# Down projections in parts of 6, 8 and 8 pairs, and the table of attention bias made during layer 0's up projection

## The chip, the cores and the metric

The kernel runs on one core of one Trainium2 chip. The metric is the device time of one execution in microseconds (us). Three runs of the kernel before took 1335.24, 1335.5 and 1338.54 us; their median, 1335.5, is the time that the change is measured against.

## The reference, cut to what matters

A trunk of two layers, for one sequence of 512 tokens of width 1024, all in fp32. Layer 0 is a Mamba-2 mixer and a ConvFFN. Then keys and values are projected once. Layer 1 is a differential attention over them, and a ConvFFN. Two pieces bear on the change: the ConvFFN of both layers (FFN width 2816), and the attention's table of bias, which depends on the distance of two tokens alone.

```python
def conv_ffn(x, ln_g, up_w, conv_w, conv_b, down_w):
    u = causal_dwconv(rms_norm(x, ln_g) @ up_w, conv_w, conv_b)
    gate, up = u[..., :FFN_DIM], u[..., FFN_DIM:]
    return (jax.nn.silu(gate) * up) @ down_w
...
    dist = qpos[:, None] - kpos[None, :]
    bias = rel_bias[t5_bucket(dist)].astype(jnp.float32).transpose(2, 0, 1)
    logits = jnp.einsum('bqhcd,bkhcd->bhcqk', qblk, k).astype(jnp.float32) * scale
    logits = logits + bias[None, :, None]
    logits = jnp.where(dist >= 0, logits, -jnp.inf)
...
        ff = conv_ffn(x, ffn_ln_g[layer], ffn_up_w[layer], ffn_conv_w[layer],
                      ffn_conv_b[layer], ffn_down_w[layer])
        x = x + ff.astype(x.dtype)
```

rel_bias has 32 buckets for each of 8 heads; t5_bucket gives every distance up to 15 a bucket of its own and shares the others out by ranges.

## The kernel before, in words

**Products.** TensorE (PE) multiplies in fp32r. For fp32 accuracy each operand is split into a high half (wh, xgh, sh) and a low half (wl, xgl, sl), and each product is made of three: wh·xh, wh·xl and wl·xh (helper mm3, L205 to L208). The halves of a weight chunk are made on the chip: ScalarE (ACT) writes the high half with a copy, VectorE (DVE) the low half with a subtraction.

**The order of the weights.** A list written at the start, `plan` (L69 to L120), names every weight chunk in the order in which PE will use it. `chunk(key)` hands out the next one and sees to it that two more (AHEAD = 2) are already split behind it. A raw chunk is loaded on SyncE's (SP's) queue into one of three buffers.

**The ConvFFN.** `ffn(l, ...)` (L954) serves both layers. The FFN's 2816 columns are 22 "pairs", each 128 gate and 128 up columns. Pairs come in parts (`PARTS_D`, L32: 8, 8 and 6). For each pair of a part, PE makes the gate and up products from two weight chunks, 48 matmuls; DVE and ACT apply the convolution's taps (L977 to L982), SiLU (L1223) and the multiplication (L1227); then `operands` (L1052 to L1080) forms, for each two pairs (a "quad"), seven sums of halves of the activations for a Strassen-like product, each in a high and a low half (sh, sl). Their buffers hold four quads.

Behind a part's last pair comes its down product. Instead of eight block products it makes seven, in the order of `SEVEN` (L33): 5, 1, 2, 6, 7, 4, 3 in layer 0 and 1, 2, 5, 7, 6, 3, 4 in layer 1. In layer 0 `down_features` (L1160) makes each of the seven from two weight chunks (14 chunks in a part), in banks of PSUM named ps_s; its matmuls are at L1186, L1188 and L1189, 6 for each quad and chunk and half of columns, so 24 a chunk with four quads and 18 with three. DVE adds the finished products to the residual stream xT (L1168) and to a running sum (L1205). In layer 1 `down_tokens` (L1082) does the same by tokens, adds to xr (L1100), and in the last part cuts the very last product (L1094, banks `end`) and stores the output as it goes.

**The down weights.** For the seven products sums of weight blocks are needed. `ahead` (L1010), called at the third pair of a part, marks the buffers behind that pair's activations (POOL copies, L1016), loads a block on SP's queue (L1017), and adds a second block to it with accumulating DMAs on GpSimd's (POOL's) queue (`plus`, L1007). `combine` (L1021) splits such a sum when its turn in `plan` comes (ACT L1035, DVE L1036) and then issues the next accumulation into the same buffer wz, for a later product. The accumulations for the first products of a part are thus issued while the up products run, and the one for the part's fourth product behind the split of the first.

**The end of layer 0.** In its last part each finished piece of xT calls `ended`: ACT and DVE split it for the key projection (xgh, xgl, L500 to L503), ACT squares it (L576), POOL sums the squares (L577) and DVE folds them (nacc_kv, L579), for the key norm, which a short chain of small DVE operations ends (L511, then L257 to L265).

**The transition into layer 1.** `proj` (L1262) multiplies the key, query and value weights, four token banks at a time, with chunks wr_k, wr_q, wr_v whose halves are made at L171 and L172. `qk` (L1285) empties each bank (ACT, knk L1293), squares it into one buffer (ACT, ksq L1294) and sums the squares (DVE, ssk L1295). Ahead of this, when the attention section begins, the table of bias is made: rb is loaded on POOL's queue (L1245), POOL copies its 32 columns into the ranges of distance, 18 copies in two tiles bv (L1255), and two DMAs on the same queue write it to the DRAM tile bd (L1256). For each head `Unit.logits` loads the table's rows from bd in a shifted form on SP's queue (tr, L1339, one buffer), and DVE reverses them into tb (L1340, two buffers).

**Who orders what.** Each engine runs its instructions in the order in which the scheduler has put them; a wait at the head of an engine's row holds all that is behind it. The same holds for the DMA issues on SP's and POOL's queues.

Of the kernel before, what the change touches and what calls it, by code (L numbers as in the profile page):

```python
# [9 lines left out]
F32 = mybir.dt.float32  # L10
# [8 lines left out]
P = 128  # L19
# [9 lines left out]
FFN = 2816  # L29
NPAIR = FFN // P  # L30
HALF = 12
PARTS_D = (0, 8), (8, 16), (16, 22)  # L32
SEVEN = "5126743", "1257634"  # L33
AH = 8
EPS = 1e-6
NEG = -1.0e30
LAM_INIT = 0.8 - 0.6 * math.exp(-0.3 * 1)
NBIAS = 640
# [3 lines left out]
def trunk_kernel(ctx: ExitStack, tc, x, ssm_ln_g, ssm_in_w, ssm_conv_w, ssm_conv_b, ssm_dt_bias,  # L42
# [4 lines left out]
    act, dve, pool, pe, sync = nc.scalar, nc.vector, nc.gpsimd, nc.tensor, nc.sync  # L47
# [9 lines left out]
    dp = ctx.enter_context(tc.tile_pool(name="scratch", bufs=1, space=DRAM))  # L57
# [33 lines left out]
    def ffn_plan(l):  # L91
        for p0, p1 in PARTS_D:
            for p in range(p0, p1):
                plan.append(("g%d_%d" % (l, p), *w_cols(ffn_up_w[l], 0, KB, p * P, P)))
                plan.append(("u%d_%d" % (l, p), *w_cols(ffn_up_w[l], 0, KB, FFN + p * P, P)))
            nq = (p1 - p0) // 2
            for m in SEVEN[l]:
                for c in range(0, nq, 2) if l else range(2):
                    plan.append(("s%d%s_%d_%d" % (l, m, p0, c), (l, m, p0, c, min(2, nq - c) if l else nq)))
# [168 lines left out]
    with tc.tile_pool(name="ph0", bufs=1) as p0:  # L268
# [153 lines left out]
        for l in range(2):  # L422
            for j in range(2):
                sfc = slice(j * FFN, (j + 1) * FFN)
                d = sf[:, 2 * l + j, :]
# [525 lines left out]
        run(out_proj(NG - 1, *prev, norm))  # L951


    def ffn(l, norm, bp, gnext, nnext):  # L954
        with tc.tile_pool(name="ffn_h%d" % l, bufs=1) as hp, tc.tile_pool(name="ffn%d" % l, bufs=1) as fp:
            rr = []

            def products(j, p, c=None):
                key = "%s%d_%d" % ("gu"[j], l, p)
                wh, wl = chunk(key)  # L960
                ps = mm_bank("ps_" + key)
                for k in range(KB):
                    last = mm3(ps, wh[:, k, :], wl[:, k, :], xgh[k], xgl[k], k == 0, k == KB - 1)
                    if c is not None and k == KB - 2:
                        with tc.issue_after(last):
                            rr.append(norm.row(c))
                return ps

            def taps(j, p, ps):
                key = "%s%d_%d" % ("gu"[j], l, p)  # L970
                r = rr[0]
                col = lambda t: cf[l][:, 88 * j + 22 * t + p:88 * j + 22 * t + p + 1]
                u = fp.tile([P, T], F32, tag="u", name="u" + key, bufs=3)
                v = fp.tile([P, T], F32, tag="v%d" % j, name="v" + key, bufs=3 if j else 4)
                if nnext is None and key in ("g1_1", "u1_1"):
                    residual(j)
                dve.tensor_tensor(out=u, in0=ps, in1=r, op=ALU.mult)  # L977
                act.activation(v, u, AF.Identity, bias=col(3), scale=col(2))
                for s in range(1, 3):
                    dve.scalar_tensor_tensor(out=v[:, s:], in0=u[:, :T - s], scalar=col(2 - s),  # L980
                                             in1=v[:, s:], op0=ALU.mult, op1=ALU.add)
                return v  # L982
# [16 lines left out]
            def source(p0, c, nq, j, i):  # L999
                p0, i = (p0 + 2 * c, i) if l else (p0, 2 * c + i)  # L1000
                src = ffn_down_w[l][p0 * P:(p0 + 2 * nq) * P, i * ncol:(i + 1) * ncol]
                return src.rearrange("(k j p) c -> j p k c", j=2, p=P)[j]

            def view(t, nq):
                return t[:, :nq * ncol].rearrange("p (k c) -> p k c", k=nq)

            def plus(t, p0, c, nq, j, i):  # L1007
                pool.dma_start(view(t, nq), source(p0, c, nq, j, i), accum_op=ALU.add)  # L1008

            def ahead(p0, n, behind):  # L1010

                for k, j, i in (("z", 0, 0), ("x", 0, 1), ("y", 1, 1)) if l else (("x", 0, 0), ("z", 0, 1)):
                    for c in range(0, n // 2, 2) if l else range(2):
                        nq = min(2, n // 2 - c) if l else n // 2
                        t = raws[k][c // 2 if l else c]
                        pool.tensor_copy(t[:, 0:1], behind[:, 0:1])  # L1016
                        sync.dma_start(view(t, nq), source(p0, c, nq, j, i))  # L1017
                        if k == "z" and not l:
                            plus(t, p0, c, nq, 1, 1)
# [195 lines left out]

            for p0, p1 in PARTS_D:
                sides = []
                for p in range(p0, p1):
                    ps = [products(0, p)]
                    if not rr:  # L1220
                        ps.append(products(1, p, norm.col()))
                    ga = taps(0, p, ps[0])
                    act.activation(ga, ga, AF.Silu)  # L1223
                    if len(ps) == 1:
                        ps.append(products(1, p))
                    up = taps(1, p, ps[1])
                    dve.tensor_tensor(out=ga, in0=ga, in1=up, op=ALU.mult)  # L1227
                    operands(p, ga, sides)
                    if p == p0 + 2:
                        ahead(p0, p1 - p0, ga)  # L1230
                (down_tokens if nnext is None else down_features)(p0, p1 - p0, sides, p1 == NPAIR)

    norm_kv = Norm(bp, "kv")
    ffn(0, norm, bp, None, norm_kv)


    norm1 = Norm(bp, "f1")
    with tc.tile_pool(name="att_o", bufs=1) as op_, tc.tile_pool(name="att", bufs=1) as ap:
        rts = []
        late = []  # L1240


        rb = ap.tile([AH, 32], F32, name="rb")
        bd = dp.tile([AH, NBIAS], F32, name="bd")
        pool.dma_start(rb, rel_bias.rearrange("b h -> h b"))  # L1245
        hb = NBIAS // 2
        for i in range(2):
            bv = ap.tile([AH, hb], F32, tag="p1", name="bv%d" % i, bufs=3)
            if i == 0:
                pool.memset(bv[:, 0:P - 1], NEG)  # L1250
            for b, a, e in _ranges():
                a, e = max(a - i * hb, 0), min(e - i * hb, hb)
                if a < e:
                    src = rb[:, 0:e - a] if b == 0 else rb[:, b:b + 1].to_broadcast([AH, e - a])
                    pool.tensor_copy(bv[:, a:e], src)  # L1255
            pool.dma_start(bd[:, i * hb:(i + 1) * hb], bv)  # L1256

        kT = [ap.tile([P, 4, T], F32, name="kT%d" % i) for i in range(2)]
        qT = [ap.tile([P, 4, T], F32, name="qT%d" % i) for i in range(2)]
# [213 lines left out]
        with tc.manual_schedule(engines={mybir.EngineType.PE}):  # L1473
# [90 lines left out]
            last_out(norm1)  # L1564

    ffn(1, norm1, bp, None, None)


def _ranges():
    dist = np.arange(NBIAS - (P - 1))  # L1570
    nf = np.maximum(dist, 1).astype(np.float32)
    large = 16 + (np.log(nf / np.float32(16)) / np.float32(math.log(8)) * np.float32(16)).astype(np.int32)
    bucket = np.where(dist < 16, dist, np.minimum(large, 31))
    at = P - 1 + np.searchsorted(bucket, np.arange(33))
    return [(0, P - 1, int(at[16]))] + [(b, int(at[b]), int(at[b + 1])) for b in range(16, 32)]
# [27 lines left out]
```

## Time and profile before

| | |
|---|---|
| runs of before (us) | 1335.24, 1335.5, 1338.54; median 1335.5 |
| the profiled execution's own time | 1335.32 us |
| its span (first to last instruction) | 1333.4 us |
| instructions | 18218 |
| TensorE clock granted | 1.00 throughout |
| layer 0's up products and down parts | from 376.9 to 730.2 us, with the down parts beginning at 464.8, 592.2 and 697.8 us |
| key, query and value projections and attention | from 730.2 us |
| layer 1's last down part | 1297.7 us to the end |

A line of the profile gives times in us from the span's start or as sums. In a group of instructions "out<-in" are the names of the tiles in the program, then come partitions x elements, a count, and in square brackets or behind the bar the idle time of that engine just before, with the instruction that ended it. A line "PE ps_q L1271 <- ACT knk L1293: 3.2, 1, 3.2" of the waits says who waited, for what, the sum of its idle time, how often, and the longest. A line of the transfers gives the size and the median time from issue to landing. A line of a table of stretches begins with the stretch and its length, and then has busy time and number of instructions of PE, PE's weight loads, DVE, ACT and POOL, the granted clock, the DMA share and GB/s.

### The profile page before, as it was taken

Reading aid. Unit: us, or ns where it says so; the run is one execution under the profiler, and the core shown is the slowest. Engines: PE = TensorE matmul, PEld = TensorE weight load, DVE = VectorE, ACT = ScalarE, POOL = GpSimd, SP = SyncE. Lnnn points to the kernel's source line nnn. Section 1 sums busy time; section 2 is a strip of 40 time slices with the busy share of each in tenths; the row PEclk is TensorE's granted clock in tenths of the full one; section 3 lists DMA queues with packets and bytes.
Section 4 is the critical chain, followed back from the end, with each engine's and each line's share of the span. In section 5 each row is a group of like instructions: output and inputs, shape, how many; then the busy total and the mean of one; then the engine's idle time right before and its main releaser. Section 6 shows DMA issues by size and latency. Waiting matters only on the chain.

```text
span 1333.4 us, 18218 instructions
## 1 busy us (share of the span) xinstructions
PE 1318.6 (99%) x6795; PEld 1100.3 (83%) x6795; DVE 1074.8 (81%) x1814; ACT 700.5 (53%) x1150; POOL 153.1 (11%) x210
## 2 busy tenths in 40 slices
PE   9999999999999999999998899999999999999998
PEld 8878888888888898889888787777788888888886
DVE  7989888789878886888789556777777987888788
ACT  6696553752444443544446455777654443454443
POOL 4330300200111010111013200000020010001001
PEclk9999999999999999999999999999999999999999
DMA  7553533432337463745365432221136353544444
GB/s 207 161 151 96 147 99 111 135 95 72 95 94 180 104 129 111 190 95 130 108 147 107 119 98 85 73 78 56 54 89 187 97 112 101 184 111 80 126 134 111
DMA packets 196024, 155.25 MB, mean 116 GB/s; under 512 B 7196, under 2 KB 175520, under 8 KB 195936
## 3 DMA queue, kind: packets, MB, share of 16 engines
q1 hardware_dynamic: 173904, 120.73, 30.8%
q0 software_dynamic: 20752, 32.26, 12.8%
q8 instruction: 53, 0.87, 0.3%
q10 hardware_dynamic: 1280, 1.10, 0.3%
q14 instruction: 35, 0.29, 0.1%
HBM read 151.83 MB, written 2.25 MB: 116 GB/s over the span
## 4 chain that ended last, share of the span: by engine, by line
PE 89%; DVE 6%; DMA 2%; ACT 1%; issue 1%; POOL 0%; SPq 0%; DVEq 0%; ACTq 0%
PE ps_g L207 5%; PE ps_u L207 5%; PE ps_u L206 5%; PE ps_g L208 5%; PE ps_g L206 5%; PE ps_u L208 5%; PE ps_in L206 5%; PE ps_in L208 5%; PE ps_in L207 5%; PE ps_s L1188 2%; PE ps_s L1189 2%; PE ps_s L1186 2%; PE ps_s L1094 2%; PE ps_o L207 2%; PE ps_o L206 2%; PE ps_o L208 2%
## 5 line engine op out<-in xcount | busy, mean ns | idle before, releaser
L206 PE MATMUL ps_u<-xgh,wh_u 128*128 128x512 f32 x352 | 137.4, 390 | 0.0
L207 PE MATMUL ps_g<-xgl,wh_g 128*128 128x512 f32 x352 | 137.1, 389 | 0.0
L206 PE MATMUL ps_g<-xgh,wh_g 128*128 128x512 f32 x352 | 137.1, 389 | 0.0
L208 PE MATMUL ps_u<-xgh,wl_u 128*128 128x512 f32 x352 | 137.0, 389 | 0.0
L208 PE MATMUL ps_g<-xgh,wl_g 128*128 128x512 f32 x352 | 137.0, 389 | 0.0
L207 PE MATMUL ps_u<-xgl,wh_u 128*128 128x512 f32 x352 | 137.0, 389 | 0.0
L206 PE MATMUL ps_in<-xgh,wh_in 128*128 128x512 f32 x304 | 123.0, 404 | 0.0
L208 PE MATMUL ps_in<-xgh,wl_in 128*128 128x512 f32 x304 | 119.8, 394 | 0.0
L207 PE MATMUL ps_in<-xgl,wh_in 128*128 128x512 f32 x304 | 119.2, 392 | 0.0
L207 PEld LDWEIGHTS ps_g<-xgl,wh_g 128*128 128x128 f32 x352 | 66.2, 188 | 13.9 <-DVE xgl L486 0.3
L208 PEld LDWEIGHTS ps_u<-xgh,wl_u 128*128 128x128 f32 x352 | 66.1, 188 | 13.8
L1189 PE MATMUL ps_s<-sl,wh_s 128*128 128x256 f32 x308 | 77.4, 283 | 0.0
L1188 PE MATMUL ps_s<-sh,wh_s 128*128 128x256 f32 x308 | 77.4, 283 | 0.0
L206 PEld LDWEIGHTS ps_g<-xgh,wh_g 128*128 128x128 f32 x352 | 66.1, 188 | 13.7
L208 PEld LDWEIGHTS ps_g<-xgh,wl_g 128*128 128x128 f32 x352 | 66.1, 188 | 13.6
L207 PEld LDWEIGHTS ps_u<-xgl,wh_u 128*128 128x128 f32 x352 | 66.1, 188 | 13.5
L206 PEld LDWEIGHTS ps_u<-xgh,wh_u 128*128 128x128 f32 x352 | 66.1, 188 | 13.5
L1008 POOL DMA_DIRECT2D wz<-in_ffn_down_w_dram x36 | 43.7, 1255 | 290.3 <-DVE wl_s L1036 224.2
L1079 ACT ACTIVATE sh<-vg 128x256 fp32r<-128x256 f32 (+1 forms) x44 | 23.0, 524 | 98.2 <-DVE vg L1227 98.1
L1223 ACT ACTIVATE vg<-vg 128x512 f32<-128x512 f32 x44 | 27.8, 633 | 88.6 <-DVE vg L980 88.6
L977 DVE TENSOR_TENSOR uu<-ps_u,nr_f 128x512 f32<-128x512 f32 x44 | 30.4, 691 | 52.3 <-PE ps_u L208 52.2
L146 ACT ACTIVATE wh_u<-wr_u 128x1024 fp32r<-128x1024 f32 x44 | 46.7, 1062 | 44.0 <-PE ps_g L207 36.1
(398 smaller groups left out, 3509.0 us busy)
## 6 DMA issues: line engine op xcount, KB each, us to landing
wr_g<-in_ffn_up_w_dram SPq DMA_DIRECT2D x44, 512.0 KB, 3.9
wr_u<-in_ffn_up_w_dram SPq DMA_DIRECT2D x44, 512.0 KB, 3.9
wr_in<-in_ssm_in_w_dram SPq DMA_DIRECT2D x40, 512.0 KB, 3.9
wz<-in_ffn_down_w_dram POOLq DMA_DIRECT2D x27, 512.0 KB, 6.5
m<-cumd POOLq DMA_DIRECT2D x16, 512.0 KB, 4.7
wr_out<-in_ssm_out_w_dram SPq DMA_DIRECT2D x16, 512.0 KB, 3.5
wr_s<-in_ffn_down_w_dram SPq DMA_DIRECT2D x13, 512.0 KB, 3.8
xT<-in_ffn_down_w_dram SPq DMA_DIRECT2D x10, 512.0 KB, 7.7
```

The lines of the kernel that those rows point to most:

```text
L146: return act.activation(self.wh[:, :self.n], self.raw[:, :self.n], AF.Copy)
L206: pe.matmul(ps, wh, xh, start=start, stop=False)
L207: pe.matmul(ps, wh, xl, start=False, stop=False)
L208: return pe.matmul(ps, wl, xh, start=False, stop=stop).ins
L977: dve.tensor_tensor(out=u, in0=ps, in1=r, op=ALU.mult)
L1008: pool.dma_start(view(t, nq), source(p0, c, nq, j, i), accum_op=ALU.add)
L1079: act.activation(sh[:, o], v, AF.Copy)
L1094: pe.matmul(pss[b], h, ws[q][1][:, cols], start=False, stop=end and q == qs[-1])
L1186: pe.matmul(v[:, b], wl[:, q, cols], h, start=False, stop=q == nq - 1)
L1188: pe.matmul(v[:, b], wh[:, q, cols], h, start=q == 0, stop=False)
L1189: pe.matmul(v[:, b], wh[:, q, cols], w, start=False, stop=False)
L1223: act.activation(ga, ga, AF.Silu)
```

## The change

Two edits. The parts of the down projection are 6, 8 and 8 pairs in place of 8, 8 and 6, in both layers. And the making of the bias table leaves the attention section for layer 0's ConvFFN, where it is called behind the fourth pair (p = 3); it is held until that pair's activations are there by a copy of one of their columns into rb, on POOL, ahead of rb's load. Its tiles rb and bv now lie in the ConvFFN's pool; bv has two tiles of its own.

```diff
-PARTS_D = (0, 8), (8, 16), (16, 22)
+PARTS_D = (0, 6), (6, 14), (14, 22)
...
+    bd = dp.tile([AH, NBIAS], F32, name="bd")
+
+    def bias_ranges(pl, behind):
+        rb = pl.tile([AH, 32], F32, name="rb")
+        pool.tensor_copy(rb[:, 0:1], behind[:AH, 0:1])
+        pool.dma_start(rb, rel_bias.rearrange("b h -> h b"))
+        hb = NBIAS // 2
+        for i in range(2):
+            bv = pl.tile([AH, hb], F32, name="bv%d" % i)
+            if i == 0:
+                pool.memset(bv[:, 0:P - 1], NEG)
+            for b, a, e in _ranges():
+                a, e = max(a - i * hb, 0), min(e - i * hb, hb)
+                if a < e:
+                    src = rb[:, 0:e - a] if b == 0 else rb[:, b:b + 1].to_broadcast([AH, e - a])
+                    pool.tensor_copy(bv[:, a:e], src)
+            pool.dma_start(bd[:, i * hb:(i + 1) * hb], bv)
...
                     if p == p0 + 2:
                         ahead(p0, p1 - p0, ga)
+                    if not l and p == 3:
+                        bias_ranges(fp, ga)
...
-        rb = ap.tile([AH, 32], F32, name="rb")
-        bd = dp.tile([AH, NBIAS], F32, name="bd")
-        pool.dma_start(rb, rel_bias.rearrange("b h -> h b"))
...
-            bv = ap.tile([AH, hb], F32, tag="p1", name="bv%d" % i, bufs=3)
...
-            pool.dma_start(bd[:, i * hb:(i + 1) * hb], bv)
```

The lines of the changed kernel lie 18 further in ffn and 4 further in the attention section (L1016 is L1034, L1036 is L1054, L1340 is L1344).

**POOL at the third and fourth pair of layer 0.** Before, the marking copies of `ahead` (for wz_1 the last of four) are followed by the accumulations, first those of the first products (2 rows), then those issued behind the splits:

```order
L1016 COPY wz_1_3660<-vg_2_3893 128x1
L1008 DMA wz_0_3659<-in_ffn_down_w_dram 128x4x256
L1008 DMA wz_1_3660<-in_ffn_down_w_dram 128x4x256
L1008 DMA wz_0_3659<-in_ffn_down_w_dram 128x4x256
L1008 DMA wz_1_3660<-in_ffn_down_w_dram 128x4x256
```

Now, in the changed kernel, the table stands there (rb's marking copy, its load, the 18 copies, of which the first and the last are shown, and the two DMAs to bd):

```order
L1034 COPY wz_1_3661<-vg_2_3894 128x1
L1026 DMA wz_0_3660<-in_ffn_down_w_dram 128x3x256
L1026 DMA wz_1_3661<-in_ffn_down_w_dram 128x3x256
L958 COPY rb<-vg_3_3988 8x1
L959 DMA rb<-in_rel_bias_dram 8x32x1
L969 COPY bv_4042<-rb 8x16
...
L969 COPY bv_4062<-rb 8x320
L970 DMA bd<-bv_4042 8x320
L970 DMA bd<-bv_4062 8x320
L1026 DMA wz_0_3660<-in_ffn_down_w_dram 128x3x256
L1026 DMA wz_1_3661<-in_ffn_down_w_dram 128x3x256
```

The table has moved ahead of the accumulations for the first part's fourth product; those have three quads in place of four. From POOL's row behind the key norm's last sum (nsum, L577) it is gone. Only the memset of bv's first tile goes further ahead, to layer 0's norm before the ConvFFN.

**DVE at the beginning of the key projection.** Before, from the last small operation of the key norm (tr_nkv, L265), with the weight splits for the query projection (wl_q), the two reversed copies of the table (tb) and the first sum of squares of the keys (ssk):

```order
L265 SCALAR_TENSOR_TENSOR tr_nkv<-rst_nkv,tr_nkv 128x4
L172 SCALAR_TENSOR_TENSOR wl_q_0_6990<-wr_q_0_6987,c_89,wh_q_0_6989 128x512 x2
L1340 COPY tb_7384<-tr_7385 128x512
L172 SCALAR_TENSOR_TENSOR wl_q_2_7022<-wr_q_2_7019,c_89,wh_q_2_7021 128x512 x2
L1340 COPY tb_7539<-tr_7540 128x512
L1295 TENSOR_REDUCE ssk_6896<-ksqk_0_7040 128x8
```

In the changed kernel, from the fold of the key norm's last sums (nacc_kv) and the last key split on:

```order
L579 TENSOR_TENSOR nacc_kv<-nsum_3665 128x256
L172 SCALAR_TENSOR_TENSOR wl_k_4_6937<-wr_k_4_6934,c_89,wh_k_4_6936 128x512 x2
L1344 COPY tb_7385<-tr_7386 128x512
L511 TENSOR_REDUCE tr_nkv<-tr_nkv 128x4
...
L265 SCALAR_TENSOR_TENSOR tr_nkv<-rst_nkv,tr_nkv 128x4
L1344 COPY tb_7540<-tr_7541 128x512
L172 SCALAR_TENSOR_TENSOR wl_q_0_6991<-wr_q_0_6988,c_89,wh_q_0_6990 128x512 x2
L172 SCALAR_TENSOR_TENSOR wl_q_2_7023<-wr_q_2_7020,c_89,wh_q_2_7022 128x512 x2
L1299 TENSOR_REDUCE ssk_6897<-ksqk_0_7041 128x8
```

The first copy of the table stands ahead of the key norm's reduction (L511), the second ahead of both query splits; before, both stood behind the norm, between and behind the query splits. On SP the load of the first tr now stands ahead of that of the query weights' third chunk (wr_q_4), before it stood behind.

**DVE at the end of layer 0's last down part.** Before, with three quads, the last two splits of down weights (wl_s, 768 elements) and what lies between and behind them: additions to xT and the low halves of the finished pieces (xgl):

```order
L1036 TENSOR_TENSOR wl_s_16_0_6726<-wz_0_3659,wh_s_16_0_6725 128x768
L503 TENSOR_TENSOR xgl<-xT,xgh 128x2x256
L1168 TENSOR_TENSOR xT<-xT,ps_s_16_0_6729 128x2x256
L1036 TENSOR_TENSOR wl_s_16_1_6755<-wz_1_3660,wh_s_16_1_6754 128x768
L1168 TENSOR_TENSOR xT<-xT,ps_s_16_1_6758 128x2x256
```

Now, with four:

```order
L1054 TENSOR_TENSOR wl_s_14_0_6729<-wz_0_3660,wh_s_14_0_6728 128x1024
L503 TENSOR_TENSOR xgl<-xT,xgh 128x2x256
L1186 TENSOR_TENSOR xT<-xT,run_sum_3666 128x2x256 x2
L1186 TENSOR_TENSOR xT<-xT,ps_s_14_0_6732 128x2x256
L503 TENSOR_TENSOR xgl<-xT,xgh 128x2x256
L1054 TENSOR_TENSOR wl_s_14_1_6764<-wz_1_3661,wh_s_14_1_6763 128x1024
L503 TENSOR_TENSOR xgl<-xT,xgh 128x2x256
```

The last splits have 1024 elements in place of 768; the additions of a finished running sum stand behind the split of 14_0 where they stood ahead of it, and otherwise the rows are the same.

PE's rows have the same matmuls as before, up to the parts: 252 in each layer 0 part of six pairs and 336 in each of eight.

More of the change, by code (lines that the diff above doesn't have):

```diff
@@ L1240, in trunk_kernel @@
         late = []
-        rb = ap.tile([AH, 32], F32, name="rb")
-        bd = dp.tile([AH, NBIAS], F32, name="bd")
-        pool.dma_start(rb, rel_bias.rearrange("b h -> h b"))
-        hb = NBIAS // 2
-        for i in range(2):
-            bv = ap.tile([AH, hb], F32, tag="p1", name="bv%d" % i, bufs=3)
[L1249 to L1256, printed above, removed]
         kT = [ap.tile([P, 4, T], F32, name="kT%d" % i) for i in range(2)]
```

## The prediction

> **What bounds the kernel.** I read the page first, for the busy time of each engine.
>
> ```profile
> span 1333.4 us, 18218 instructions
> PE 1318.6 (99%) x6795; PEld 1100.3 (83%) x6795; DVE 1074.8 (81%) x1814; ACT 700.5 (53%) x1150; POOL 153.1 (11%) x210
> ```
>
> PE is busy for 1318.6 of 1333.4 us. The change leaves PE every matmul it had (order prints 6002 rows for PE before and after), so there are only 15 us of idle PE and the tail behind its last matmul to win. The view of waits says whom PE waits for.
>
> ```profile
> PE ps_q L1271 <- ACT knk L1293: 3.2, 1, 3.2
> PE ps_k L1272 <- DVE wl_k L172: 2.7, 2, 1.7
> PE ps_s L1186 <- DVE wl_s L1036: 1.6, 2, 0.9
> ...
> PE ktk L1309 <- issue: 0.4, 1, 0.4
> ```
>
> These are 7.9 us in six waits, and in order of time they stand within 45 us: the end of layer 0's last down part (ps_s L1186), the first key projection (ps_k), the first query projection (ps_q, ktk). Each wait costs a little more than its idle time, for a matmul runs 0.39 us and the next one normally starts 0.23 us after it: 0.16 us of overlap are lost each time, 1.0 us in all. **Layer 0's end costs 8.9 us.** The columns of the next rows, of the down parts' instructions alone, are the stretch, its length, and busy time with the number of instructions of each engine.
>
> ```profile
> 465.00:505.00 40.00, 40.00 (x335) 40.00 (x335) 10.19 (x15) 1.16 (x2) 1.00 0.64 129
> 697.80:730.20 32.40, 30.73 (x252) 30.28 (x252) 9.51 (x14) 1.18 (x2) 1.00 0.58 117
> 1069.20:1107.20 38.00, 38.00 (x168) 31.30 (x167) 8.98 (x14) 1.18 (x2) 1.00 0.49 95
> 1297.70:1328.30 30.60, 29.46 (x123) 22.32 (x122) 8.87 (x14) 1.17 (x2) 1.00 0.47 95
> ```
>
> A part of eight pairs runs without a gap: 0.119 us a matmul in layer 0, 0.226 in layer 1. A part of six, which here is each layer's last, does not: 252 matmuls at 0.119 are 30.0 us and take 32.4; in layer 1, 123 at 0.226 and six half-width ones at 0.12 are 28.5 and take 30.6, so 2.1 us are lost there too, most of it too short for the list of waits.
>
> **The bias table.** Its stall is seen in DVE's rows behind the key projection, with ACT's and POOL's beside them.
>
> ```profile
> 740.87 0.41 DVE L579 TENSOR_TENSOR nacc_kv<-nsum 128x256 f32<-128x256 f32 x1
> ...
> 742.30 0.69 DVE L511 TENSOR_REDUCE tr_nkv<-tr_nkv 128x4 f32<-128x512 f32 x1 [0.35 <-PE tr_nkv L509]
> ...
> 745.85 1.42 DVE L172 SCALAR_TENSOR_TENSOR wl_q<-wr_q,c,wh_q 128x512 fp32r<-128x512 f32 x2 [0.48 <-ACT wh_q L171]
> 755.92 0.43 DVE L1340 COPY tb<-tr 128x512 f32<-128x512 f32 x1 [8.65 <-DMA tr<-bd]
> ```
> ```profile
> 751.89 0.69 ACT L1293 ACTIVATE knk<-ps_k,tr_nkv 128x512 f32<-128x512 f32 x1
> ...
> 760.55 0.63 ACT L1294 ACTIVATE ksqk<-knk 128x512 f32<-128x512 f32 x1 [6.66 <-DVE ssk L1295]
> ```
> ```profile
> 742.05 0.78 POOL L1245 DMA_DIRECT2D rb<-in_rel_bias_dram  x1 [4.18 <-DVE wl_k L172]
> ...
> 746.52 3.13 POOL L1255 COPY bv<-rb 8x16 f32<-8x16 f32 x18 [3.51 <-DMA rb<-in_rel_bias_dram]
> 749.61 1.08 POOL L1256 DMA_DIRECT2D bd<-bv  x2
> ```
> ```profile
> wz<-in_ffn_down_w_dram POOLq DMA_DIRECT2D x6, 384.0 KB, 6.5
> tr<-bd SPq DMA_DIRECT2D x8, 256.0 KB, 3.1
> ```
>
> POOL cannot begin the table before 742.05 and hands it over at 750.7; the copy of its first rows holds DVE's queue 8.65 us. Behind it stand the sums of squares (ssk); ACT, which empties the key banks (knk) and squares them (ksqk), has one buffer for the squares and waits 6.66 us, so a bank of key products is not emptied, and PE waits its 3.2 us. With the table made 300 us earlier, this chain has no start: the 3.2, the 0.4 of ktk behind it and two overlaps, 3.9 us, go.
>
> Is DVE free of the copy now? In the new order the first copy stands ahead of the norm's reduction (order rows above). Its load may start when the norm's last sums (nacc_kv) are done, at 741.3 in the old time, and takes 3.1 us (the median, last row): 744.4. The copy's 0.43 end at 744.8. The reduction it holds up stood at 742.30, with small operations behind it until 745.4; 2.5 us later they end at 747.9. The first key bank is emptied at 751.89, so 4 us are spare, and more when layer 0's end loses less. On SP the weight load wr_q_4 stands behind that load; it asks for a buffer that the last key split frees at about the same time. I count nothing, with the old 3.9 us as the other end.
>
> **The parts in layer 0.** What makes the last part late is DVE.
>
> ```profile
> 697.80:730.20 32.40, 30.77 (x254) 30.33 (x253) 32.13 (x47) 21.55 (x32) 8.93 (x7) 1.00 0.58 117
> 697.80:742.00 44.20, 39.90 (x293) 37.29 (x293) 43.88 (x62) 28.51 (x42) 13.11 (x9) 1.00 0.54 120
> L1036 DVE TENSOR_TENSOR wl_s<-wz,wh_s 128x1024 fp32r<-128x1024 f32 x32 | 38.7, 1223 | 2.8 <-ACT wh_s L1035 2.5
> L1036 DVE TENSOR_TENSOR wl_s<-wr_s,wh_s 128x768 fp32r<-128x768 f32 x4 | 3.8, 948 | 0.0
> ```
> ```profile
> 727.15 1.46 DVE L1036 TENSOR_TENSOR wl_s<-wz,wh_s 128x768 fp32r<-128x768 f32 x1
> ```
>
> DVE (third engine) is busy 43.88 of 44.20 us, through the part and into the key projection. With four quads in place of three PE has 336 - 252 = 84 matmuls more, 10.0 us, over the part's 14 chunks; DVE has the same instructions, of which twelve splits grow by 1.22 - 0.95 = 0.27 us: 3.2 us. Its last split (the row at 727.15) ends 30.8 us into the part, where a PE without waits comes to it after 13 × 18 + 6 = 240 matmuls, 28.6 us: 2.2 late. Now it ends at 34.0, and PE comes after 13 × 24 + 8 = 320 matmuls, 38.1 us: a lead of 4 us. The key splits behind it, late by at most 2 us, gain as much. All of 1.6 + 2.7 us and four overlaps, 4.9, should go; I leave 0.4 for a wait of PE that shows then. A rest that stays: POOL's norm additions slow DVE here.
>
> ```profile
> 729.34 3.30 POOL L577 TENSOR_TENSOR nsum<-nsum,nsq_kv 128x512 f32<-128x512 f32 x2 [1.55 <-ACT nsq_kv L576]
> 729.73 1.77 DVE L172 SCALAR_TENSOR_TENSOR wl_k<-wr_k,c,wh_k 128x512 fp32r<-128x512 f32 x1
> ```
>
> A split of 0.71 us (two in 1.42, above) takes 1.77 beside such an addition; this is in the 43.88 already.
>
> The part of six is now the first. There DVE lacks what is special to the end: eight subtractions for xgl at 0.68 us, five of them inside the old window (3.4 us), and the slowing by POOL (0.5 in the split at 727.15 alone). 32.1 - 3.9 + 1.2 for one more weight split = 29.4 us of DVE stand against PE's 30.0; it just holds. Bounds: nothing, or the 2.4 us of the old last part. I take nothing; PE's order in the first six-pair part is that of the old last part up to the fourth product, so no queue differs.
>
> **The table's new place on POOL.** It stands between the accumulating transfers of the first down part.
>
> ```profile
> 415.47 0.51 POOL L1016 COPY wz<-vg 128x1 f32<-128x1 f32 x2
> ...
> 425.89 1.28 POOL L1008 DMA_DIRECT2D wz<-in_ffn_down_w_dram  x1 [0.19 <-issue]
> ...
> 670.24 0.51 POOL L1016 COPY wz<-vg 128x1 f32<-128x1 f32 x2
> ...
> 689.28 1.25 POOL L1008 DMA_DIRECT2D wz<-in_ffn_down_w_dram  x1 [8.45 <-DVE wl_s L1036]
> ```
> ```profile
> 706.36 0.85 ACT L1035 ACTIVATE wh_s<-wz 128x768 fp32r<-128x768 f32 x1 [0.58 <-ACT sh L1079]
> ```
>
> The old last part has the new first part's form, 254.8 us later (670.24 - 415.47). So POOL is free at 427.2, and the next accumulation is due at 689.28 - 254.8 = 434.5. The table takes 0.3 (a copy that waits for pair 3's product: 48 matmuls, 10.9 us, behind pair 2's, which released the row at 415.47, so it is there) + 8.6 (742.05 to 750.7) = 8.9 us: it ends at 436.1, and behind it the accumulation is 1.6 us late. It lands 6.5 us after its issue (the median above), at 442.6; ACT reads it at 706.36 - 254.8 = 451.6. Nine microseconds cover it, so nothing is paid. DVE loses at most the 3.1 us of the copies, in a stretch where it is busy 18.27 of 22.00 us:
>
> ```profile
> 443.00:465.00 22.00, 22.00 (x100) 18.23 (x99) 18.27 (x26) 10.73 (x15) 2.53 (x2) 1.00 0.36 79
> L1016 POOL COPY wz<-vg x12: 177/277/396, 415.5 to 1270.3; 128x1 f32<-128x1 f32 x12
> ```
>
> The small copies on POOL were taken with DVE idle (0.17 us each). Beside a busy DVE the nearest row has 0.28 at the median, so 18 take 5.0 us. The far bound is that each first waits for one of DVE's 1.22 us splits: 25 us. I take 5.0, which moves the end to 438.0. The Trainium skill ("SBUF — State Buffer", section "SBUF: two separate sides") speaks against the move: VectorE and GpSimd share a pair of ports that one instruction locks for its whole length. The 1.77 us above agree with such blocking; the 0.28 us say that a small copy does not pay for a whole instruction of DVE's, and by the rule taken at its worst the far bound would hold.
>
> **The parts in layer 1.** The six-pair losses move from last to first: 2.1 us go and about the same come; at the first part's end DVE must also split the next up weights (1.22 each), so I set 2.4. The eight-pair last part keeps 0.3 at its final split. The tail shortens:
>
> ```profile
> 1328.01 0.39 PE L1094 MATMUL end<-wl_s,sh 128*128 128x256 f32 x2
> ```
> ```profile
> 1327.20 2.48 DVE L1100 TENSOR_TENSOR xr<-xr,ps_s 128x512 f32<-128x512 f32 x4
> 1329.78 0.75 DVE L1100 TENSOR_TENSOR xr<-xr,end 128x256 f32<-128x256 f32 x2
> ```
>
> DVE ends at 1330.5, 2.5 us after PE's last matmuls began, because it is still adding earlier products. Two products of PE (36 matmuls before) last 2.7 us longer with four quads, DVE's two splits 0.5 longer: the four earlier additions are then done in time but for one, and DVE ends about 1.2 us after. Gain 1.3. Layer 1: -2.1 + 2.4 + 0.3 - 1.3 = -0.7, bounds -3.4 and +1.5.
>
> **Sum.** Against the profiled execution's 1335.3 us (span 1333.4 and 1.9 around it): -3.9 (bias) - 4.9 + 0.4 (layer 0's end) - 0.7 = -9.1, 1326.2. That execution lies 0.2 below the median of 1335.5, so I say **1326.3 us**, and 1323.6 (layer 1 at its lower bound) to 1328.9 (its upper bound, and another 0.4 at layer 0's end) as this case's own range.
>
> **Rivals.**
> - *A new wait for the old.* The copy now ahead of the reduction comes so late that the key banks wait, as they did. For: DVE still stops at it. Against: 4 us of spare time. If 3.9 us stay: 1330.2.
> - *Six pairs are too few for DVE anywhere.* Layer 0's first part loses 2.4, as its last did (32.13 of 32.40), the key splits stay half late (2), layer 1 gives nothing. Against: the end's extra work is gone. 1326.3 + 2.4 + 2 + 0.7 = 1331.4, on the line between faster and same.
> - *The table blocks POOL.* Place: ahead of the accumulation for the first part's fourth product. PE asks for it at 443.1 + 108 × 0.119 = 455.9, and with the table's end at E it is split at E + 6.5 + 0.85; from E = 448.5 each us costs one. At the far bound of the copies, E = 458, 9.5 us are lost and nothing is won: 1335.8, the same. **Slower** needs E past 458, over 31 us where 8.6 were measured; at 463 it gives 1340.8. Against it: 0.28 us a copy, and 3.5 us for rb's load. By the skill's port rule alone E is 458 at worst.
> - *The change does nothing*: the stalls are set elsewhere. Against: each row above names its releaser.
>
> **Chances.** Forecast 0.72; new wait 0.07; six too few 0.11, half of it on each side; POOL blocked or nothing changed 0.06; slower 0.04. About 0.3%, 4 us, is what a measurement of this kernel can tell from no change: faster 0.85, same 0.11, slower 0.04. The range goes from the forecast's low end, 1323.6, to the second rival's 1331.4.
>
> **What would show it.** Right: PE's waits of ps_s for wl_s, of ps_k for wl_k and of ps_q for knk gone; tb's copies without 8 us of idle DVE; table copies on POOL near 432 to 437 and none near 746; the first six-pair part of layer 0 in 30.0 us; PE's sum of idle time near 7 us. Wrong: PE waiting in the first down part for a wz split (POOL), 32 us for that part (DVE), or knk's wait still there with the norm's chain as its cause.

## The result, and the profile after

Four runs of the changed kernel took 1323.43 to 1324.30 us, median 1323.99, beside 1335.37 for four runs of the kernel before: a ratio of 0.9909, 95% interval 0.9892 to 0.9926, or 11.4 us by the medians and 12.1 by the ratio. The forecast was 9.2 us. The direction held, and the waits went that were to go; they were worth more than the sum said, and by the ratio (0.9909 of 1335.5 is 1323.3) the time lies 0.3 us below the stated range.

The changed kernel's page, and PE's waits (in total, times, longest):

```profile
span 1322.5 us, 18212 instructions
PE 1316.6 (100%) x6795; PEld 1100.8 (83%) x6795; DVE 1074.1 (81%) x1814; ACT 701.2 (53%) x1150; POOL 158.8 (12%) x211
```
```profile
PE warm L290 <- DVE ones L217: 1.1, 1, 1.1
PE ps_s L1112 <- DVE wl_s L1054: 0.7, 1, 0.7
```

All six waits that the forecast counted are gone, ktk's 0.4 among them. One new wait stands in layer 1. All engines in the stretch from layer 0's last splits to the end of the query projection, first of before, then of the change:

```profile
725.00:769.00 44.00, 36.14 (x172) 28.80 (x171) 29.67 (x55) 21.51 (x36) 11.87 (x26) 1.00 0.35 104
```
```profile
725.00:769.00 44.00, 44.00 (x220) 37.12 (x219) 28.31 (x53) 22.32 (x37) 5.08 (x3) 1.00 0.39 126
```

PE was busy for 36.14 us of it (172 matmuls) and now for all 44.00 (220).

**The table.** POOL's row in the changed kernel, in its new place:

```profile
422.79 2.69 POOL L1026 DMA_DIRECT2D wz<-in_ffn_down_w_dram  x2 [6.43 <-DMA wz<-in_ffn_down_w_dram]
426.22 0.43 POOL L958 COPY rb<-vg 8x1 f32<-8x1 f32 x1 [0.74 <-DVE vg L1245]
...
432.50 5.39 POOL L969 COPY bv<-rb 8x16 f32<-8x16 f32 x18 [4.77 <-DMA rb<-in_rel_bias_dram]
437.85 1.08 POOL L970 DMA_DIRECT2D bd<-bv  x2
438.92 2.68 POOL L1026 DMA_DIRECT2D wz<-in_ffn_down_w_dram  x2
```

The copies took 5.39 us (5.0 expected), and the table ends at 438.9 (438.0). PE waits for none of it. At the other end, DVE's and then ACT's rows at the key projection:

```profile
735.71 1.41 DVE L172 SCALAR_TENSOR_TENSOR wl_k<-wr_k,c,wh_k 128x512 fp32r<-128x512 f32 x2
739.99 0.43 DVE L1344 COPY tb<-tr 128x512 f32<-128x512 f32 x1 [2.88 <-DMA tr<-bd]
740.33 0.69 DVE L511 TENSOR_REDUCE tr_nkv<-tr_nkv 128x4 f32<-128x512 f32 x1
...
743.24 0.17 DVE L265 SCALAR_TENSOR_TENSOR tr_nkv<-rst_nkv,tr_nkv 128x4 f32<-128x4 f32 x1
```
```profile
745.49 1.34 ACT L171 ACTIVATE wh_q<-wr_q,c 128x512 fp32r<-128x512 f32 x2 [4.05 <-PE ps_k L1277]
746.89 0.69 ACT L1297 ACTIVATE knk<-ps_k,tr_nkv 128x512 f32<-128x512 f32 x1
```

The copy now ahead of the norm holds DVE for 2.88 us (8.65 before). The norm's scale is ready at 743.4, and the first key bank is emptied at 746.89, behind a split that waited for PE: 3.5 us are spare, so the copy costs nothing.

**The down parts.** All engines in layer 0's first part, and in layer 1's first part, of six pairs each (third is DVE):

```profile
443.45:473.68 30.23, 30.23 (x254) 30.23 (x252) 30.03 (x44) 15.68 (x20) 5.04 (x4) 1.00 0.67 132
1038.20:1068.50 30.30, 29.57 (x129) 23.70 (x128) 28.89 (x42) 15.62 (x20) 4.26 (x4) 1.00 0.44 89
```

In layer 0 PE has no gap, with DVE busy 30.03 of 30.23 us: by the busy time it just holds (the experiment with more work for DVE finds some slack). In layer 1 PE loses 0.7 us to the new wait, and 1.35 in all when each matmul's distance to the next is set against the median of its kind. In the tail DVE's last additions now end at 1319.6, 0.9 us behind PE's last matmul (2.1 before):

```profile
1318.04 0.69 DVE L1118 TENSOR_TENSOR xr<-xr,ps_s 128x512 f32<-128x512 f32 x1 [0.49 <-PE ps_s L1112]
1318.83 0.75 DVE L1118 TENSOR_TENSOR xr<-xr,end 128x256 f32<-128x256 f32 x2
```

### The profile page after: what moved, and what is told of

The parts are those of the page before. It is cut to its first block, busy times and chain, and to the rows that moved or that the text cites. A ratio compares the mean times of both kernels' runs of the same rounds, so it can differ in the third digit from the quotient of the medians.

```text
span 1322.5 us, 18212 instructions
## 1 busy us (share of the span) xinstructions
PE 1316.6 (100%) x6795; PEld 1100.8 (83%) x6795; DVE 1074.1 (81%) x1814; ACT 701.2 (53%) x1150; POOL 158.8 (12%) x211
```

## The experiments

Two measures are used. The times are medians, beside runs of the kernel before on the same chip (median 1336.3 in the first two sets, 1335.9 in the third). The stages are taken from one trace each, between the starts of layer 0's first gate product, the first key product and layer 1's first gate product, the end of PE's last matmul, and the span's end; they are free of the start of the program, whose first gate product came anywhere from 376.3 to 378.1 us. In us:

| kernel | layer 0's ConvFFN | key product to layer 1's ConvFFN | layer 1's ConvFFN | tail |
|---|---|---|---|---|
| before, first profile | 353.33 | 247.19 | 351.01 | 5.02 |
| before, four more | 353.34 to 353.74 | 247.35 to 248.56 | 349.96 to 350.26 | 5.01 to 5.04 |
| changed | 351.21 | 239.74 | 350.53 | 3.76 |
| parts alone, two profiles | 351.21, 351.21 | 244.89, 244.57 | 350.45, 350.76 | 3.97, 3.96 |
| table alone | 353.31 | 243.00 | 350.24 | 5.01 |
| 6, 8, 8 in layer 0 alone, and the table | 351.21 | 239.72 | 350.07 | 5.01 |

**The parts alone** (before's code, with the new list):

```diff
-PARTS_D = (0, 8), (8, 16), (16, 22)
+PARTS_D = (0, 6), (6, 14), (14, 22)
```

> Parts of 6, 8 and 8 pairs in both layers, the bias table made in its old place, at the start of the attention section. Theory (the two edits remove separate stalls): the waits for wl_s and wl_k at layer 0's end go as in the changed kernel, and PE's wait for knk behind the first table copy stays, 3.2 us and about 0.7 around it. The key splits that release the table end about 3 us earlier, but PE's key products do too. Time 1324.0 + 3.9 = 1327.9 us. Rival (the table is late only because layer 0's end is late): with the end mended the wait for knk is gone, time 1324.0.

Measured: 1328.33 us (1327.55 to 1329.77), ratio 0.9941 [0.9929, 0.9953]. Of the six waits only that for the table stays:

```profile
PE ps_q L1271 <- ACT knk L1293: 3.3, 1, 3.3
PE warm L290 <- DVE ones L217: 1.1, 1, 1.1
```

The rival is out: mending layer 0's end does not mend the table's stall. The theory's 1327.9 was near.

**The table alone** (the changed code, with the old list).

> Parts of 8, 8 and 6 pairs as before, the bias table made early as in the changed kernel. Theory: only the wait for knk and that of ktk behind it go, 3.9 us; the waits for wl_s (1.6) and wl_k (2.7) stay, and so does layer 1's last part. Time 1335.4 - 3.9 = 1331.5 us. Rival (the late key splits, not the table, hold knk): nothing moves, 1335.4.

Measured: 1330.58 us (1330.06 to 1332.22), ratio 0.9960 [0.9948, 0.9973].

```profile
PE ps_k L1276 <- DVE wl_k L172: 2.7, 2, 1.7
PE ps_s L1204 <- DVE wl_s L1054: 1.6, 2, 0.9
```

The two edits remove separate stalls, as forecast. But the saving, 5.7 us by the medians and 4.2 by the stage (247.19 - 243.00), is more than 3.9.

**The new parts in layer 0 only.**

```diff
-PARTS_D = (0, 6), (6, 14), (14, 22)
+PARTS_D = ((0, 6), (6, 14), (14, 22)), ((0, 8), (8, 16), (16, 22))
...
-        for p0, p1 in PARTS_D:
+        for p0, p1 in PARTS_D[l]:
...
-            for p0, p1 in PARTS_D:
+            for p0, p1 in PARTS_D[l]:
```

> The changed kernel with layer 1's parts put back to 8, 8 and 6; layer 0 keeps 6, 8 and 8 and the early table. By the profiles of before and of the change, layer 1's order of parts is worth 0.5 us up to PE's last matmul and 1.2 us in the tail behind it: 1324.0 + 1.7 = 1325.7 us. By the sum of the prediction it is worth 0.7: 1324.7. Rival (the saving beyond the sum came from layer 0 or the attention): 1324.0 to 1324.7.

Measured: 1324.12 us, ratio 0.9911 [0.9898, 0.9925]. My 1325.7 was wrong: it took layer 1's 351.01 from the first profile of before, which is 0.8 us slower than any other trace with this order. Layer 1 and tail are 355.08 us here and 354.29 in the changed kernel: by these two traces its order of parts is worth 0.8, near the prediction's 0.7. The two medians, 0.1 us apart, are too close to show it.

**The part of six in the middle of layer 0** (8, 6, 8), layer 1 as changed.

> The changed kernel with the six-pair part of layer 0 in the middle: 8, 6, 8 in layer 0, 6, 8, 8 in layer 1. Theory (the part of six was late only for the end's extra work on DVE): a part of six without that work runs in 30.1 us, the key projection starts without a wait, time 1324.0 us. Rival (six pairs give DVE too little time for a part's splits and additions wherever they stand, and the first part escapes because fewer other things run beside it): the middle part takes 32.4 us as the old last one did, time 1326.3.

Measured: 1323.75 us, ratio 0.9906 [0.9892, 0.9919].

```profile
569.85:600.20 30.35, 30.35 (x254) 30.34 (x253) 30.15 (x44) 15.81 (x20) 5.07 (x4) 1.00 0.64 127
```

The middle part of six runs without a gap, as the theory had it; only as the last part, with the end's extra work on DVE, was it late.

**The part of six in the middle of layer 1** (8, 6, 8), layer 0 as changed.

> The changed kernel with layer 1's six-pair part in the middle: 8, 6, 8. In the changed kernel the first part of six loses 1.35 us at its end, where DVE is busy without a gap and the next up splits stand behind. Theory (six pairs are too few for DVE in layer 1 wherever an up projection follows): the middle part loses the same, 1324.0 us. Rival (what is special to the first part costs it): the middle one runs clean, 1322.7 us.

Measured: 1324.06 us, ratio 0.9907 [0.9894, 0.9921]. As the theory had it, the wait stands in the middle part now, and layer 1 takes 350.53 us again:

```profile
PE ps_s L1112 <- DVE wl_s L1054: 0.5, 1, 0.5
```

**More work for DVE** in layer 0's first part (six pairs), and in its last (eight), behind products 1, 2 and 6. The first of the two kernels is shown; the second has p0 == 14:

```diff
+            more = None if l else fp.tile([P, 2, 256], F32, name="more")
...
+                        if p0 == 0 and m in "126":
+                            x_ = xTt[:, 4 * c:4 * c + 2, 256 * (m == "6"):256 * (m == "6") + 256]
+                            dve.tensor_tensor(out=more, in0=x_, in1=x_, op=ALU.mult)
```

> The changed kernel with six more DVE multiplications of 128x512 (0.68 us each, 4.1 in all, into a tile that nobody reads) between the additions of products 1, 2 and 6 of layer 0's first down part, that of six pairs. Theory (six pairs leave DVE no slack: busy 30.03 of 30.23 us there): nearly all of it becomes time, 1324.0 + 3.9 = 1327.9 us, as waits of PE for wl_s in that part or for the gate and up splits behind it. Rival (the splits are two chunks ahead, and DVE catches up in the up products): 1324.0 to 1325.

> The same six multiplications in layer 0's last down part, that of eight pairs. By the changed kernel's trace its last split ends 3.0 us ahead of PE and DVE waits 0.8 us for PE late in the part; so the waits for wl_s stay away, while the key splits behind, with a lead of 1.3 us, come up to 2 us late: 1324.0 + 1 to 2 = 1325.5 us. Rival (eight pairs give no lead that counts): 1324.0 + 4 = 1328.0. Rival (DVE is nowhere near the bound): 1324.0.

Measured: 1326.69 us (0.9925 [0.9913, 0.9937]) and 1326.81 us (0.9927 [0.9916, 0.9939]). First the waits of the first, then those of the second:

```profile
PE ps_u L206 <- ACT wh_u L146: 0.8, 1, 0.8
...
PE ps_s L1207 <- ACT wh_s L1053: 0.6, 1, 0.6
PE ps_g L206 <- ACT wh_g L146: 0.2, 1, 0.2
```
```profile
PE ps_k L1279 <- DVE xT L1187: 1.5, 2, 0.9
...
PE ps_k L1280 <- DVE wl_k L172: 0.3, 1, 0.3
```

By the stages 4.1 us of DVE cost 2.3 in the part of six (353.55 against 351.21) and 2.7 in the key projection behind the part of eight (242.43 against 239.74). So the part of six has 1.8 us of slack with what follows it, more than its busy time says; and with more work for DVE it is late, as the old last part was. The part of eight takes all 4.1 without a wait of its own, but the keys behind it, whose banks wait for the additions, do not. Both expectations were a little off, to opposite sides.

**A longer table** on POOL:

```diff
+            for k in range(48 if i == 0 else 0):
+                pool.tensor_copy(bv[:, P - 1:P + 15], rb[:, 0:16])
```

> The changed kernel with 48 more copies of 8x16 on POOL into the table (0.30 us each there, 14.4 in all, written before it leaves and with values that differ there), so that the table ends at about 453.3 us in place of 438.9, and the accumulations for the first part's fourth product are issued behind it. By the prediction each us beyond an end of 448.5 (448.9 in the changed kernel's time) costs one: 4.4 us, 1328.4, and 1.6 more if the wait brings a half clock. Rival (the accumulations are not needed so early, or the copies do not hold POOL's queue): 1324.0. Rival (copies hold DVE): several us of DVE's wait on top, spread over the up products.

Measured: 1336.36 us, ratio 1.0001 [0.9992, 1.0010]: the whole saving is gone. POOL's row, PE's wait, and the clock (the last column but two) before and behind it:

```profile
438.53 17.50 POOL L971 COPY bv<-rb 8x16 f32<-8x16 f32 x43
456.37 1.31 POOL L1028 DMA_DIRECT2D wz<-in_ffn_down_w_dram  x1 [0.34 <-issue]
```
```profile
PE ps_s L1208 <- ACT wh_s L1055: 10.1, 1, 10.1
```
```profile
452.60:463.00 10.40, 0.27 (x4) 0.06 (x2) 2.52 (x5) 0.90 (x2) 9.09 (x18) 0.64 0.77 153
463.00:468.00 5.00, 5.00 (x23) 5.00 (x24) 2.12 (x3) 1.75 (x3) 1.26 (x2) 0.50 1.21 189
```

The mechanism of the third rival is real, but the point from which it costs lies nearer than I put it. The copies took 0.40 us each, not 0.30. PE began to wait at 452.6, after 84 matmuls of the part, not after 108 at 455.5: its row has four high products of the fourth product's first chunk ahead of the third product's low ones, which I had counted first. The accumulation was issued at 456.4 and PE lost 10.3 us at the wait. If each us of delay costs one, the loss begins with an issue at 446.1, 3.5 us into the part. The changed kernel issues at 438.9, 4.5 us ahead of the part, so 8 us are spare, where I had 10.5. And 2.7 us more went to matmuls at half the clock.

**The last additions of layer 1's first part on POOL** (four of xr and run_sum, product 6).

```diff
-                def add(t, v, op=ALU.add):
-                    dve.tensor_tensor(out=t, in0=t, in1=v, op=op)
+                def add(t, v, op=ALU.add, eng=dve):
+                    eng.tensor_tensor(out=t, in0=t, in1=v, op=op)
...
-                            add(to(2 + b, 512), r, ALU.subtract)
-                            add(to(2 + b, 0), r)
+                            eng = dve if p0 else pool
+                            add(to(2 + b, 512), r, ALU.subtract, eng)
+                            add(to(2 + b, 0), r, ALU.add, eng)
```

> The changed kernel with the four last additions of a running sum to xr (2.5 us on DVE, product 6, layer 1's first part of six pairs) made on POOL. Theory (DVE's row at that part's end, four additions ahead of the last two splits, makes the splits late): the wait for wl_s goes, 1.35 us, 1322.7 us. Rival (POOL's additions slow DVE beside them by as much, as its norm sums did with 1.77 us for a split of 0.71): 1324.0 or more.

Measured: 1324.22 us, ratio 0.9907 [0.9892, 0.9922]: as the changed kernel, and as the rival had it. POOL's row, then DVE's:

```profile
1062.69 7.54 POOL L1118 TENSOR_TENSOR xr<-xr,run_sum 128x512 f32<-128x512 f32 x4 [3.81 <-DVE run_sum L1118]
```
```profile
1063.65 3.10 DVE L1054 TENSOR_TENSOR wl_s<-wz,wh_s 128x1024 fp32r<-128x1024 f32 x2 [0.46 <-ACT wh_s L1053]
...
1069.01 2.31 DVE L157 TENSOR_TENSOR wl_u<-wr_u,wh_u 128x1024 fp32r<-128x1024 f32 x1
```

DVE gives 2.5 us away and gets 1.3 back as slower splits beside POOL's additions (two in 3.10 us, against 1.83 in the changed kernel) and 1.1 in the up split at their end (2.31 against 1.23). PE's wait moves to the gate's split.

**Where the missing two us were.** In the first profile of the parts alone eight matmuls behind the wait for knk stood 0.43 us apart in place of 0.23. Two kernels shorten and lengthen that wait. The first gives all far distances the value of bucket 23, so its table is another there; the second only repeats copies:

```diff
-            for b, a, e in _ranges():
+            for b, a, e in _ranges()[:8] + [(23, _ranges()[8][1], NBIAS)]:
```
```diff
+            for k in range(24 if i == 0 else 0):
+                pool.tensor_copy(bv[:, P - 1:P + 15], rb[:, 0:16])
```

> Parts of 6, 8 and 8 pairs, the table late, but made with 10 copies in place of 18: the last eight buckets' ranges beyond bucket 23 take bucket 23's value, so the table's far distances differ. The copies take about 1.2 us less and PE's wait for knk should be 2.1 us in place of 3.3. Theory A (a wait of PE of more than about 3.2 us makes the chip grant the clock at half for some 3.7 us, eight matmuls at 0.43 in place of 0.23 us, 1.6 us on top, in some executions): no half clock in any execution, 1328.1 - 1.2 = 1326.9 us, the five runs within 1 us of each other. Theory B (the half clock in the profile of the parts alone was chance, without a link to the wait): as often as there, one run in five near 1328.5.

> Parts of 6, 8 and 8 pairs, the table late, with 24 more copies of 8x16 into the table (0.17 us each, 4.2 in all, written before it leaves and with values that differ there): PE's wait for knk should be 7.5 us in place of 3.3. Theory A (half clock behind a long wait): in every execution 8 or more matmuls at 0.43 us behind the wait, 1328.1 + 4.2 + 1.6 = 1333.9 us. Theory B (chance): 1328.1 + 4.2 = 1332.3 us.

Measured: 1325.88 us (1325.73 to 1327.65) and 1335.18 us (1334.39 to 1336.39). In the profile of the short one the wait is gone altogether, for the copies took 1.9 us less and POOL waited 2.0 us for rb's load where it had waited 3.4; there is no half clock. Its spread is no smaller than that of the parts alone. Its slowest run, 1327.65 us, has a mean granted clock of 0.998, the other four 0.999 or 1.000, so a half clock in that one is likely, but it has no trace. In the long one the mean clock is 0.996 in all eleven runs, as theory A had it; the time is 1.3 us over its 1333.9, for PE waits 8.7 us and not 7.5. Behind that wait the granted clock is half for 4.9 us:

```profile
752.80:761.90 9.10, 0.41 (x3) 0.02 (x1) 3.38 (x6) 1.21 (x2) 0.00 (x0) 0.70 0.63 184
761.90:766.80 4.90, 4.90 (x12) 3.84 (x13) 3.05 (x7) 3.40 (x7) 0.00 (x0) 0.50 0.09 22
```

Then the kernel before was profiled four more times, and the parts alone once more:

> The kernel before, profiled once more. The first profile has the wait for knk at 3.2 us and no half clock behind it. Theory A (a wait of that length brings half a clock in some executions): either the same as there, or eight matmuls or so at 0.43 us behind the wait and about 1.6 us more. Theory B (the price of the old stall is the 3.9 us of the first profile in every execution): the same wait and no half clock.

> The kernel before, a third profile. If the half clock is part of what the old waits usually cost, there are 6 to 12 matmuls at 0.43 us behind the waits for wl_k or for knk and 1.2 to 2.4 us more than in the first profile between layer 0's last down part and the values' projection; if it is rare, none, and that stretch takes what it took in the first profile.

> The kernel before, a fourth profile. The same two expectations as for the third: 6 to 12 matmuls at 0.43 us in the transition if the half clock is usual, none if it is rare.

> The kernel before, a fifth profile. The same two expectations as for the third: 6 to 12 matmuls at 0.43 us in the transition if the half clock is usual, none if it is rare.

> Parts of 6, 8 and 8 pairs with the table late, a second profile. Its first has a wait of 3.3 us for knk and eight matmuls at 0.43 us behind it, in the slowest of five runs. If the half clock is usual behind such a wait, it is there again; if it comes only where the wait covers some window of the clock's own, it may be gone, and the time is 1.6 us less.

The times of these five executions were 1336.34, 1335.23, 1336.04, 1335.75 (before) and 1329.28 us (parts alone). Matmuls at half clock stood in three of the four, and in the parts alone again: six behind the key splits in the second profile of before, eight behind knk in the fourth, in the fifth and in the parts alone. PE's rows in the second profile of before, with start, duration and, in brackets, the waits:

```profile
732.24 0.50 PE L1272 MATMUL ps_k<-wl_k,xgh 128*128 128x512 f32 x1 [0.97 <-DVE wl_k L172]
732.57 0.39 PE L1273 MATMUL ps_k<-wh_k,xgl 128*128 128x512 f32 x1
732.80 0.40 PE L1271 MATMUL ps_k<-wh_k,xgh 128*128 128x512 f32 x1
734.93 0.80 PE L1272 MATMUL ps_k<-wl_k,xgh 128*128 128x512 f32 x1 [1.73 <-DVE wl_k L172]
735.53 0.63 PE L1273 MATMUL ps_k<-wh_k,xgl 128*128 128x512 f32 x1
735.95 0.63 PE L1271 MATMUL ps_k<-wh_k,xgh 128*128 128x512 f32 x1
```

In the first three rows the matmul that waited starts at 732.24, the next 0.33 us after it, and the third 0.23 after that, which is the usual distance. Behind every wait at full clock but ktk's the next matmul comes 0.1 us late in this way.

The fourth and the first profile of before, a stretch with the wait for knk and one behind it:

```profile
758.80:762.60 3.80, 0.43 (x2) 0.01 (x1) 1.59 (x3) 1.20 (x2) 0.00 (x0) 1.00 0.68 213
763.90:767.30 3.40, 3.40 (x10) 2.58 (x9) 2.36 (x5) 2.34 (x7) 0.00 (x0) 0.50 0.00 0
```
```profile
758.20:761.80 3.60, 0.41 (x2) 0.00 (x0) 1.60 (x3) 1.20 (x2) 0.00 (x0) 1.00 0.66 207
761.80:767.00 5.20, 5.19 (x22) 4.17 (x23) 3.31 (x9) 3.94 (x9) 0.00 (x0) 1.00 0.10 29
```

Behind a wait of 3.4 us the clock was 0.50 in one, and 1.00 behind 3.2 us in the other (as behind 3.4 in the third profile). Runs without a trace say how usual this is: of the 41 runs of before beside the experiments, 32 have a mean clock of 0.998 or less. Of the six traces of before and the changed kernel, the two with so low a mean both had a half clock near these waits (so did one with 0.999, since the mean takes in the whole span); of the 4 runs of the changed kernel none is below 0.999. The Trainium skill ("TensorE: Matmul & The Clock Gate", section "Part 1: The HAM clock gate (the "warmup" mystery)") says that TensorE falls to half its clock after an idle window of about 3.4 us, and that the windows run free of the program. That executions of one kernel differ agrees with it, and so does the length of the slow time (3.4 us at 0.50). But in the second profile PE was busy for three matmuls between two waits of 0.97 and 1.73 us and the clock still fell, and in the fourth it fell 1.3 us after PE had resumed: here the window did not have to be idle throughout. The same two short waits left the clock full in the other four profiles of before and in that of the table alone, so a wait's length does not decide it by itself.

## Why the prediction was right or wrong

1. *What bounds the kernel, and which waits go*: right. All six are gone. The two kernels with one edit each put five of them down to the edit that the prediction named; ktk's 0.4 is missing with either edit, and in two of the five profiles of before.
2. *The sum for layer 0's end* (3.9 + 4.9 - 0.4 = 8.4): too small, and the step that failed is the price of a wait in it, "0.16 us of overlap are lost each time", worked out from one execution. The sum forecasts the first two stages of the table above, and these gave 353.33 + 247.19 - 351.21 - 239.74 = 9.6 us in the first profile of before, 10.1 to 11.3 in the other four.

   In the first profile, which the prediction used, the difference is placed: behind five of the six waits the next matmul also comes 0.1 us late, 0.5 in all; the 0.4 that I held back for a wait that would show was not needed; the last 0.3 lies in delays of under 0.1 us each. In three of the five executions there is more: behind one of the waits six or eight matmuls run at half the clock, 1.3 to 1.6 us, and the first profile was not one of those. And the wait for knk was 2.8 to 3.7 us, where I had 3.2, with POOL's wait for rb's load between 2.9 and 3.7 us.

   In three profiles of before 0.4 us more lie within layer 0's ConvFFN: three matmuls of the first gate product stand 0.34 to 0.37 us apart in place of 0.23. The kernel with the short table has nearly the same, so the edits have no part in it; why it comes and goes is left open.

   By edit: the table alone is worth 4.2 without a half clock (247.19 - 243.00) and 4.8 to 5.2 with it (the parts alone against the changed kernel), for my 3.9; the parts 2.1 + 3.3 = 5.4 (353.31 - 351.21, 243.00 - 239.74), for my 4.5.
3. *The first copy of the table ahead of the norm costs nothing*: right, with 3.5 us spare.
4. *A part of six is late only at layer 0's end*: right: the first part and the middle part run clean, and 4.1 us of added work for DVE makes the first one late by 2.3. The lead of 4 us of the part of eight was 3.4 (last split done at 723.2, PE there at 726.5), and the part of six has more slack than I gave it.
5. *The table's new place on POOL*: right to within 1 us (438.9 for 438.0), and the far bound of 25 us for the copies was not near: they took 5.39. The point from which the table would cost lies 2.5 us nearer than I worked out.
6. *Layer 1, -0.7*: right in sum (0.7 to 1.0 with the tail, against every trace of the old order but the first), but by luck, for three of its terms were off and made up for each other. The new first part loses 1.35, not 2.4. In the other four profiles of before layer 1's ConvFFN was 0.3 to 0.6 us shorter than in the changed kernel, so the old last part lost only 0.8 to 1.1 there; I had 2.1 from the first profile, which was slow at this place. The 0.3 at the new last part's final split did not show, and the tail gave its 1.3.
7. *The range*: its lower end took in only layer 1's bounds. With what the stalls gave beyond the sum, 1.2 to 2.9 us (9.6 to 11.3 for 8.4), it would have held the time with room.

## What to carry to other kernels

Here a wait of the busiest engine was worth more than its idle time in one profile: look at the clock column of the rows behind it, and profile the kernel twice or more before a sum of small stalls is made. When a DMA chain's result is waited for in an in-order queue, count what is queued behind the waiting instruction; here moving the chain ahead by some 300 us cost nothing, because the next due transfer of its engine had a lead of about 8 us. Where work is cut into unequal parts, put the smallest one where the other engines have the least to do besides.

## What the runs showed of the hardware

- TensorE's clock was granted at half for 3 to 6 us behind waits of 3.0, 3.3, 3.4, 3.7, 8.7 and 10.1 us, and once behind two short waits with 2.7 us idle in 4; it stayed full behind waits of 2.8, 3.2 and 3.4, and behind the same two short waits in five other traces. None of the eight profiles without such waits at this place shows it there.
- Behind a wait the waiting matmul's successor started 0.33 us after it in place of 0.23, at full clock.
- A POOL addition of 128x512 beside DVE's splits took 1.9 us (7.54 for four), and the splits beside it took 1.55 us on the mean, against 0.92 without it; small copies of 8x16 took 0.17 us with DVE idle (3.13 for 18) and 0.30 to 0.40 beside a busy one (5.39 for 18, 17.50 for 43).
- POOL waited for the load of rb, 1 KB, 2.0 to 3.7 us in its old place and 4.5 to 7.2 us in its new one, beside the up products.
